# A decoder trunk on one core: other openings for the split products, an earlier norm statistic, and adaLN tables moved to TensorE

## The chip, the core and the metric

The kernel runs on one core of a Trainium2 chip. The engines spoken of are TensorE (PE in the profile; PEld is its weight load), VectorE (DVE), ScalarE (ACT), GpSimd (POOL) and SyncE (SP), which here issues most of the loads. Each engine runs its own instructions in the order in which the program gives them and waits on semaphores. The metric is the device time of one execution in microseconds; the profile's times count from the first instruction of the span.

## The reference

Two layers over 256 tokens of width 2048, all in float32. Layer 0 mixes tokens with an S5 state-space layer (128 groups of 16 channels, 64 complex states each), layer 1 with an RG-LRU; after each mixer stands a SwiGLU of hidden width 5632. Every sub-layer is normalised and modulated by the conditioning vector c.

```python
cond = jax.nn.silu(c)
for i in range(DEPTH):
    mod = cond @ w_ada[i] + b_ada[i]                 # 2048 -> 6 * 2048
    sh1, sc1, g1, sh2, sc2, g2 = [m[:, None, :] for m in jnp.split(mod, N_MOD, axis=-1)]
    h = rmsnorm(x, norm_g[i, 0]) * (1.0 + sc1) + sh1
    y = s5_mixer(h, ...) if i % N_MIXERS == 0 else rglru_mixer(h, ...)
    x = x + g1 * y
    h = rmsnorm(x, norm_g[i, 1]) * (1.0 + sc2) + sh2
    x = x + g2 * swiglu(h, ffn_w_gu[i], ffn_w_down[i])
return rmsnorm(x, final_g)
```

In the S5 mixer u = h @ w_in, then per group a diagonal complex recurrence over time with input and output matrices, a GELU, and y @ w_glu, whose halves are multiplied (value by sigmoid of gate).

## The kernel before

**One stream of weights.** All weights are read once, as 1 MB tiles (`raw`, four buffers, NRAW = 4) in one written order, the list `items` in `run`. `Stream.load` issues a load on SP's queue as soon as the program comes to a step; on the chip it waits until the buffer four items back is free. `Stream.step` (L443 on) uses an item up by its kind: "w" is a weight block that is split, "f" an S5 input block used as it is, "a", "p" and "q" are adaLN tables (192 of them, 128 columns of w_ada each).

**adaLN tables.** Kind "a" is one VectorE instruction per table (L486): multiply by c and sum, one output column. Kind "p" goes through TensorE: four tables hold four row blocks of 512 columns, each table gives four matmuls at once into four strips of a bank `pa` (L494); after the fourth, ScalarE copies the bank to `par` (L500), and at the next group's second table `rows_out` turns the rows into columns with four small matmuls into `pc` (L515) and a copy into `modr` (ScalarE L507, VectorE L505 once `late` is set). The string KINDS says which table is of which kind; the host lays the tables out by it.

**Split products.** A float32 product is made of two reduced-precision parts of each operand. For each 128 x 128 block of weights ScalarE makes the high part `wh` (L467) and VectorE the low part `wl` (L482); activations are kept as x[:, 0] high and x[:, 1] low, 256 columns each. `mac` (L586) issues a pair for one block: `wl` times the high activations (256 columns, L594), then `wh` times both (512 columns, L595). `product` runs 16 or 22 pairs into one bank. With `turn`, the first pair of a product is issued the other way round (L591, L592). In the kernel before, that is so in product g of j = 1 in the first half of each FFN, in lg5, in every xb from j = 2 on, and in wo2.

**The opening and the first mixer.** `s5_layer` (L817) first goes through tables, while VectorE makes the S5 parameter tables in the generator `prep` (16 pieces up to its yields, two pieces each step), ScalarE and POOL make the sum of squares of X (`sq_add`, L659 to L664), and POOL makes matrices of group t in `gen_gl(t)` (twelve instructions; it needs buffers s5gs, of which there are two). `norm_stat` (L667) has three parts: two matmul groups that sum over channels, then the variance on VectorE (`var_s`, L680) and its power on POOL (`rs_s`, L681), then a matmul that spreads it (`nrb_s`, L685). The norm is applied to X by sixteen VectorE multiplications (L877). `gen2(t)` has TensorE transpose and multiply what `gen_gl(t)` made: its bank `pt` has one buffer, is changed by VectorE (L323) and copied by ScalarE (L327). `gen_p(t)` makes phase tables on VectorE (L290 to L293; five buffers).

Then a loop over t = 0 to 15: 16 matmuls `in` (L891) of block t of w_in, and between them the pieces of neighbouring groups: states of t - 1 (`pv` L353, then a chain on VectorE with a scan, L362 to L372, ending in `S`), outputs of t - 2 (`py`, L390 and L392, which reads S), and gen2 of t + 2. Two adaLN tables follow each block from t = 1 on. At the end of each turn stand gen_d, gen_p, a small load and gen_gl.

**After it.** `glu` (v and gt products, 32 in all), `ffn` for layer 0 (two halves of 44 products g and u, then 16 products d of 22 pairs), `lru_layer` (44 products xb and lg with the block-diagonal gates `ri` between them, whose matmuls have 256 columns each, and 16 products wo), `ffn` for layer 1, and the last norm. In `modulate` the first two products of a stage run interleaved in two banks (f_first, lru_first).

Of the kernel before, what the change touches and what calls it, by code (L numbers as in the profile page):

```python
# [29 lines left out]
def bc(ap, axis, n):  # L30

    ap = ap.unsqueeze(axis)
    shape = list(ap.shape)
    shape[axis] = n
    return ap.to_broadcast(shape)


def weight_slots(pool):
# [364 lines left out]
class Stream:  # L403
# [138 lines left out]
    def next(self):  # L542

        if not self.pieces:
            self.ahead()
        self.cur = self.pieces.pop(0)
        return self.cur[0], self.cur[1]
# [23 lines left out]
class Model:  # L571
# [11 lines left out]
                self.side.pop(0)  # L583


    def mac(self, bank, w, x, first, last, turn=False):  # L586

        mm = self.nc.tensor.matmul
        wh, wl = w
        if first and turn:  # L590
            mm(bank, wh, x, start=True, stop=False, skip_group_check=True)  # L591
            mm(bank[:, 0], wl, x[:, 0], start=False, stop=False, skip_group_check=True)  # L592
        else:
            mm(bank[:, 0], wl, x[:, 0], start=first, stop=False, skip_group_check=True)  # L594
            mm(bank, wh, x, start=False, stop=last, skip_group_check=True)  # L595

    def product(self, ps, rhs, nk, name, last=False, turn=False):


        bank = self.bank(ps, name)  # L600
        for k in range(nk):
            self.mac(bank, self.st.next(), rhs(k), k == 0, k == nk - 1, turn)
            if last in (True, "hold") and k > nk - 10:
                self.st.delay = True
            self.st.used(last in ("hold", "evict") and k == nk - 1)
        return bank
# [156 lines left out]
    def ffn(self, layer, perm, nxt):  # L763
        nc, tc = self.nc, self.tc
        with ExitStack() as c:
# [6 lines left out]
            for half in range(2):  # L772
                for j in range(22):
                    nm = f"{layer}_{half}_{j}"
                    if j == 0 and half == 0:
                        bg, bu = first
                    else:
                        bg = self.product(ps, self.rhs_h, 16, f"g{nm}", turn=(half == 0 and j == 1))
                        bu = self.product(ps, self.rhs_h, 16, f"u{nm}")
                    g = hp.tile([P, T], F32, tag="g", bufs=2, name=f"gs{nm}")  # L780
                    u = hp.tile([P, T], F32, tag="u", bufs=2, name=f"us{nm}")
                    self.halves(hp, bg, g, f"g{nm}")
                    nc.scalar.activation(g, g, AF.Silu)  # L783
                    self.halves(hp, bu, u, f"u{nm}")
                    nc.vector.tensor_tensor(u, g, u, MUL)
                    self.split(hid[:, j], u)
                    self.pump()
                if half == 0:
                    g2 = self.mods(layer, 5)
                elif nxt:  # L790
                    self.scale(*nxt)
                for m in range(16):
                    nm = f"{layer}_{half}_{m}"
                    if half == 1 and m == 15:
                        self.sq_add(14)
                    bd = self.product(ps, lambda k: hid[:, k], 22, f"d{nm}", half == 1 and m == 15)
                    if half == 1 and 0 < m < 15:
                        self.sq_add(m - 1)
                        if not nxt and m - 1 in FIN_POOL:
                            nc.scalar.activation(self.X[:, m - 1], self.X[:, m - 1], AF.Copy,  # L800
                                                 scale=self.ng[:, 4, m - 1:m])
                    x = self.X[:, m]
                    t = hp.tile([P, T], F32, tag="dt", bufs=2, name=f"dt{nm}")
                    gm = g2[:, m:m + 1]
                    nc.vector.scalar_tensor_tensor(t, bd[:, 1], gm, x, MUL, ADD)
                    if perm and half == 1:
                        nc.vector.scalar_tensor_tensor(
                            x.rearrange("p (m q) -> p q m", q=4), bd[:, 0].rearrange("p (q m) -> p q m", q=4), gm,
                            t.rearrange("p (q m) -> p q m", q=4), MUL, ADD)
                    else:  # L810
                        nc.vector.scalar_tensor_tensor(x, bd[:, 0], gm, t, MUL, ADD)
                    self.pump()
                if half == 1:
                    self.sq_add(15)


    def s5_layer(self):  # L817
# [3 lines left out]
        with ExitStack() as c:  # L821
# [23 lines left out]
            with tc.tile_pool(name="s5prep", bufs=1) as pw:  # L845
# [7 lines left out]
                    s5.load_bc(t)  # L853
                prep = s5.prep(pw)
                stat = self.norm_stat(mm, "s5")
                for i in range(16):
                    st.step()
                    for _ in range(2):
                        next(prep, None)
                    if 2 <= i < 10:  # L860
                        self.sq_add(2 * i - 4, nc.gpsimd)
                        self.sq_add(2 * i - 3, nc.gpsimd)
                    if i == 10:
                        s5.gen_gl(0)
                    if 10 < i < 13:
                        next(stat)
                    if i == 13:
                        s5.gen_gl(1)
                for _ in prep:
                    pass  # L870
            s5.work = c.enter_context(tc.tile_pool(name="s5w", bufs=1))
            next(stat, None)
            for i in range(16, 28):
                st.step()
                if i < 20:
                    for k in range(4 * i - 64, 4 * i - 60):
                        nc.vector.tensor_tensor(self.X[:, k], self.X[:, k], self.rs, MUL)  # L877
                if 20 <= i < 25:
                    s5.gen_p(i - 20)
                if i in (17, 23):  # L880
                    for f in s5.gen2((i - 17) // 6):
                        f()
                    s5.gen_gl((i - 17) // 6 + 2)
            st.late = True
            s5.load_bc(4)
            s5.gen_d(0)
# [36 lines left out]
            for t in range(16):  # L923
# [25 lines left out]
                if t == 0:  # L949
                    nc.scalar.activation(self.cond, self.cond, AF.Silu)  # L950
                s5.gen_d(t + 1)
                if 0 < t < 11 or t == 14:
                    s5.gen_p(t + 4 if t < 11 else 15)
                s5.load_bc(t + 5)
                if t != 9:
                    s5.gen_gl(t + 4 if t < 9 else t + 3)
# [18 lines left out]
    def glu(self):  # L975
        nc, ps, d, g1 = self.nc, self.ps, self.d, self.mod[:, 32:48]
        with self.tc.tile_pool(name="glu", bufs=1) as wk:
# [10 lines left out]
                nc.vector.tensor_tensor(self.X[:, m], self.X[:, m], V.pop(m), ADD)  # L988
            V[0] = self.acc
            for m in range(1, 15):  # L990
                bv = self.product(ps, self.rhs_h, 16, f"v{m}")
                if m > 1:
                    self.sq_add(m - 2)
                gate(m - 1)
# [54 lines left out]
    def lru_layer(self):  # L1049
        nc, tc, d = self.nc, self.tc, self.d  # L1050
        v, s, e = nc.vector, nc.scalar, nc.gpsimd
        with ExitStack() as c:
# [78 lines left out]
                    R[i].clear()  # L1131

            def g0(j):
                G[j]["ps"] = self.product(ps, self.rhs_h, 16, f"lg{j}", turn=(j == 5))

            spare = []

# [26 lines left out]

            def x0(j):
                if j > 1:
                    first.append(self.product(ps, self.rhs_h, 16, f"xb{j}", "evict", True))

            def xe(j):
                x = xr[j % 2]  # L1170
# [36 lines left out]
            for m in range(16):  # L1207
                if m == 14:
                    self.scale(1, 1)
                if m == 15:  # L1210
                    self.sq_add(14)
                bd = wo[m] if m < 2 else self.product(ps, lambda k: dst[k], 22, f"wo{m}", m == 15, m == 2)
                if 0 < m < 15:
                    self.sq_add(m - 1)
                x = self.X[:, m]
# [103 lines left out]

FIN_POOL = (2, 4, 6, 8, 10, 12)  # L1320

KINDS = "p" * 32 + "p" * 8 + "a" * 40 + "qqqp" + "a" * 56 + "qqqp" + "a" * 32 + "qqqp" + "a" * 12


def lru_ks(j):
# [95 lines left out]
```

## Time and profile before

| what | value |
|---|---|
| time, median of 3 runs | 2520.15 us (2510.43 to 2521.91) |
| profiled execution, its own time | 2520.73 us |
| its span | 2518.6 us, 36646 instructions |
| PE busy | 2393.6 us, 95% of the span |
| DVE busy | 1933.3 us, 77% |
| ACT, POOL busy | 1297.6 us (52%), 351.6 us (14%) |
| read from HBM | 614.57 MB, 245 GB/s over the span |
| mean granted TensorE clock | 0.977 |

"Busy" of PE counts a matmul until its modelled end, so neighbouring matmuls overlap and a PE without a gap shows as fully busy. A row of waits reads: engine, line waiting <- engine, line that ended the wait: us in total, times, longest. A row of one line's instructions reads: how many, shortest/median/longest duration in ns, first and last start. In groups the number behind the first bar is busy us, then mean ns of one, then idle time before it. A timeline row reads: start, us, engine, line, operation.

### The profile page before, as it was taken

Reading aid. Unit: us, or ns where it says so; the run is one execution under the profiler, and the core shown is the slowest. Engines: PE = TensorE matmul, PEld = TensorE weight load, DVE = VectorE, ACT = ScalarE, POOL = GpSimd, SP = SyncE. Lnnn points to the kernel's source line nnn. Section 1 sums busy time; section 2 is a strip of 40 time slices with the busy share of each in tenths; the row PEclk is TensorE's granted clock in tenths of the full one; section 3 lists DMA queues with packets and bytes.
Section 4 is the critical chain, followed back from the end, with each engine's and each line's share of the span. In section 5 each row is a group of like instructions: output and inputs, shape, how many; then the busy total and the mean of one; then the engine's idle time right before and its main releaser. Section 6 shows DMA issues by size and latency. Waiting matters only on the chain. (4 is left out here: it accounts for less than half of the span.)

```text
span 2518.6 us, 36646 instructions
## 1 busy us (share of the span) xinstructions
PE 2393.6 (95%) x14120; PEld 2054.9 (82%) x14120; DVE 1933.3 (77%) x2653; ACT 1297.6 (52%) x2520; POOL 351.6 (14%) x345
## 2 busy tenths in 40 slices
PE   5697898999999999999999988999999999999998
PEld 1276787887888888888888887888788888888887
DVE  9669887887776787777889999888777555555565
ACT  1286675445444444444446765554645444454443
POOL 5579530001000000000003333010100000000000
PEclk9799898999999999999999999999999999999999
DMA  9744555887676798776886446879777556555553
GB/s 379 283 180 176 186 207 227 322 311 279 248 258 232 269 329 322 279 282 251 307 312 222 158 157 241 316 276 324 293 285 262 182 179 209 201 199 188 172 192 134
DMA packets 98415, 619.04 MB, mean 246 GB/s; under 512 B 11201, under 2 KB 15681, under 8 KB 38977
## 3 DMA queue, kind: packets, MB, share of 16 engines
q1 hardware_dynamic: 96368, 613.04, 67.3%
q10 hardware_dynamic: 1872, 3.67, 0.4%
q8 instruction: 110, 1.80, 0.3%
q14 instruction: 65, 0.52, 0.1%
HBM read 614.57 MB, written 2.10 MB: 245 GB/s over the span
## 5 line engine op out<-in xcount | busy, mean ns | idle before, releaser
L482 DVE TENSOR_TENSOR wl<-raw,wh 128x1024 fp32r<-128x1024 f32 (+2 forms) x824 | 888.2, 1099 | 350.7 <-ACT wh L467 347.6
L467 ACT ACTIVATE wh<-raw 128x1024 fp32r<-128x1024 f32 (+2 forms) x824 | 769.6, 952 | 677.7 <-PE d L595 194.6
L595 PE MATMUL d<-hid,wh 128*128 128x512 f32 x1408 | 483.6, 391 | 0.0
L595 PE MATMUL u<-H,wh 128*128 128x512 f32 x1376 | 476.5, 390 | 0.0
L595 PE MATMUL g<-H,wh 128*128 128x512 f32 x1374 | 475.8, 391 | 0.0
L594 PE MATMUL d<-hid,wl 128*128 128x256 f32 x1408 | 391.4, 278 | 0.0
L594 PE MATMUL u<-H,wl 128*128 128x256 f32 x1376 | 382.5, 278 | 0.0
L594 PE MATMUL g<-H,wl 128*128 128x256 f32 x1374 | 382.0, 278 | 0.0
L486 DVE CUSTOM_DVE_ANT_0 raw<-raw,cond 128x2048 f32<-128x2048 f32 x140 | 327.3, 2343 | 1.1 <-DMA raw<-in_wada 0.8
L595 PEld LDWEIGHTS d<-hid,wh 128*128 128x128 f32 x1408 | 264.2, 188 | 56.8
L595 PEld LDWEIGHTS u<-H,wh 128*128 128x128 f32 x1376 | 258.3, 188 | 55.3
L595 PEld LDWEIGHTS g<-H,wh 128*128 128x128 f32 x1374 | 257.8, 188 | 55.0
L594 PEld LDWEIGHTS d<-hid,wl 128*128 128x128 f32 x1408 | 264.3, 188 | 0.0
L594 PEld LDWEIGHTS u<-H,wl 128*128 128x128 f32 x1376 | 258.3, 188 | 0.0
L594 PEld LDWEIGHTS g<-H,wl 128*128 128x128 f32 x1374 | 258.0, 188 | 0.1
L891 PE MATMUL in<-s5h,raw 128*128 128x256 f32 x512 | 149.5, 413 | 7.6 <-DMA raw<-in_s5win 6.3
L783 ACT ACTIVATE gs<-gs 128x256 f32<-128x256 f32 x88 | 36.8, 418 | 202.3 <-DVE gs L632 202.3
L595 PE MATMUL lg<-H,wh 128*128 128x512 f32 x351 | 124.2, 398 | 0.0
L891 PEld LDWEIGHTS in<-s5h,raw 128*128 128x128 f32 x512 | 91.2, 201 | 23.7 <-issue 7.8
L594 PE MATMUL lg<-H,wl 128*128 128x256 f32 x351 | 99.6, 284 | 4.5 <-DVE wl L482 4.5
L595 PE MATMUL xb<-H,wh 128*128 128x512 f32 x300 | 103.4, 390 | 0.0
L681 POOL TENSOR_TENSOR rs_lru<-var_lru,mhalf 128x2 f32<-128x2 f32 x1 | 1.6, 1600 | 729.1 <-DVE var_lru L680 729.1
(381 smaller groups left out, 3651.3 us busy)
## 6 DMA issues: line engine op xcount, KB each, us to landing
raw<-in_wada SPq DMA_DIRECT2D x192, 1024.0 KB, 5.5
raw<-in_gu SPq DMA_DIRECT2D x176, 1024.0 KB, 4.9
raw<-in_dn SPq DMA_DIRECT2D x128, 704.0 KB, 4.2
raw<-in_lruin SPq DMA_DIRECT2D x44, 1024.0 KB, 5.0
raw<-in_s5glu SPq DMA_DIRECT2D x32, 1024.0 KB, 5.6
raw<-in_lruout SPq DMA_DIRECT2D x32, 704.0 KB, 4.9
raw<-in_s5win SPq DMA_DIRECT2D x16, 1024.0 KB, 5.8
raw<-in_lruri SPq DMA_DIRECT2D x8, 512.0 KB, 5.4
```

What stands on the lines that cost most here:

```text
L467: nc.scalar.activation(dh, src, AF.Copy)
L482: self.nc.vector.tensor_tensor(*self.lazy.pop(0), SUB)
L486: self.nc.vector.tensor_tensor_reduce(t, t, self.cond, 1.0, 0.0, MUL, ADD, self.mod[:, n:n + 1])
L594: mm(bank[:, 0], wl, x[:, 0], start=first, stop=False, skip_group_check=True)
L595: mm(bank, wh, x, start=False, stop=last, skip_group_check=True)
L681: nc.gpsimd.tensor_tensor(rs, var, self.mhalf, ALU.pow)
L783: nc.scalar.activation(g, g, AF.Silu)
L891: nc.tensor.matmul(bank, st.next()[0], hf[:, k], start=(k == 0), stop=(k == 15))
```

## The change

Three edits. First, `product` takes a tuple: an order for each of its first pairs. Order 0 issues the high part as two matmuls of 256 columns and then the low part; order 1 issues the high part (512) and then the low part (256). `every(m)` gives orders (0, 1) to the first two pairs when m % 4 == 1. It is used for g in both halves of both FFNs, for d, for v, for lg, and, shifted by three, for wo; xb gets order 1 for its first pair at j = 2, 6, 10, 14 and 18 only.

Second, KINDS makes tables 40 to 59 of kind "p"; they stand behind the S5 input blocks of the loop over t.

Third, in the opening the squares are taken in steps 1 to 3 and the first two parts of `norm_stat` at step 6, ahead of that step's pieces of `prep`; gen_gl 0 and 1 are issued at steps 7 and 9; the spreading matmul follows step 13 instead of step 15; gen2 stands at steps 16 and 21 instead of 17 and 23; and two of the five gen_p there go into the loop over t.

```diff
+def every(m):
+    return (0, 1) if m % 4 == 1 else ()
...
-    def mac(self, bank, w, x, first, last, turn=False):
+    def mac(self, bank, w, x, first, last, turn=None):
...
-        if first and turn:
-            mm(bank, wh, x, start=True, stop=False, skip_group_check=True)
-            mm(bank[:, 0], wl, x[:, 0], start=False, stop=False, skip_group_check=True)
+        if turn == 0:
+            mm(bank[:, 0], wh, x[:, 0], start=first, stop=False, skip_group_check=True)
+            mm(bank[:, 1], wh, x[:, 1], start=False, stop=False, skip_group_check=True)
+            mm(bank[:, 0], wl, x[:, 0], start=False, stop=last, skip_group_check=True)
+        elif turn == 1:
+            mm(bank, wh, x, start=first, stop=False, skip_group_check=True)
+            mm(bank[:, 0], wl, x[:, 0], start=False, stop=last, skip_group_check=True)
         else:
...
-            self.mac(bank, self.st.next(), rhs(k), k == 0, k == nk - 1, turn)
+            self.mac(bank, self.st.next(), rhs(k), k == 0, k == nk - 1, turn[k] if k < len(turn) else None)
...
-                        bg = self.product(ps, self.rhs_h, 16, f"g{nm}", turn=(half == 0 and j == 1))
+                        bg = self.product(ps, self.rhs_h, 16, f"g{nm}", turn=every(j))
...
-                    bd = self.product(ps, lambda k: hid[:, k], 22, f"d{nm}", half == 1 and m == 15)
+                    bd = self.product(ps, lambda k: hid[:, k], 22, f"d{nm}", half == 1 and m == 15, every(m))
...
-                for i in range(16):
+                for i in range(14):
                     st.step()
+                    if i == 6:
+                        next(stat)
+                        next(stat)
                     for _ in range(2):
                         next(prep, None)
-                    if 2 <= i < 10:
-                        self.sq_add(2 * i - 4, nc.gpsimd)
-                        self.sq_add(2 * i - 3, nc.gpsimd)
-                    if i == 10:
-                        s5.gen_gl(0)
-                    if 10 < i < 13:
-                        next(stat)
-                    if i == 13:
-                        s5.gen_gl(1)
+                    if 1 <= i < 4:
+                        for k in range(6 * i - 6, min(6 * i, 16)):
+                            self.sq_add(k, nc.gpsimd)
+                    if i in (7, 9):
+                        s5.gen_gl((i - 7) // 2)
                 for _ in prep:
                     pass
+            next(stat, None)
             s5.work = c.enter_context(tc.tile_pool(name="s5w", bufs=1))
-            next(stat, None)
-            for i in range(16, 28):
+            for i in range(14, 28):
                 st.step()
-                if i < 20:
-                    for k in range(4 * i - 64, 4 * i - 60):
+                if i < 18:
+                    for k in range(4 * i - 56, 4 * i - 52):
                         nc.vector.tensor_tensor(self.X[:, k], self.X[:, k], self.rs, MUL)
-                if 20 <= i < 25:
-                    s5.gen_p(i - 20)
-                if i in (17, 23):
-                    for f in s5.gen2((i - 17) // 6):
+                if i in (16, 21):
+                    for f in s5.gen2((i - 16) // 5):
                         f()
-                    s5.gen_gl((i - 17) // 6 + 2)
+                    s5.gen_gl((i - 16) // 5 + 2)
+                if 22 <= i < 25:
+                    s5.gen_p(i - 22)
...
-                if 0 < t < 11 or t == 14:
-                    s5.gen_p(t + 4 if t < 11 else 15)
+                if t < 12 or t == 14:
+                    s5.gen_p(t + 3 if t < 12 else 15)
...
-                bv = self.product(ps, self.rhs_h, 16, f"v{m}")
+                bv = self.product(ps, self.rhs_h, 16, f"v{m}", turn=every(m))
...
-                G[j]["ps"] = self.product(ps, self.rhs_h, 16, f"lg{j}", turn=(j == 5))
+                G[j]["ps"] = self.product(ps, self.rhs_h, 16, f"lg{j}", turn=every(j))
...
-                    first.append(self.product(ps, self.rhs_h, 16, f"xb{j}", "evict", True))
+                    first.append(self.product(ps, self.rhs_h, 16, f"xb{j}", "evict", (1,) if j % 4 == 2 else ()))
...
-                bd = wo[m] if m < 2 else self.product(ps, lambda k: dst[k], 22, f"wo{m}", m == 15, m == 2)
+                bd = wo[m] if m < 2 else self.product(ps, lambda k: dst[k], 22, f"wo{m}", m == 15, every(m + 3))
...
-KINDS = "p" * 32 + "p" * 8 + "a" * 40 + "qqqp" + "a" * 56 + "qqqp" + "a" * 32 + "qqqp" + "a" * 12
+KINDS = "p" * 60 + "a" * 20 + "qqqp" + "a" * 56 + "qqqp" + "a" * 32 + "qqqp" + "a" * 12
```

More of the change, by code (lines that the diff above doesn't have):

```diff
@@ L595, in mac, with product @@
             mm(bank, wh, x, start=False, stop=last, skip_group_check=True)
-    def product(self, ps, rhs, nk, name, last=False, turn=False):
+    def product(self, ps, rhs, nk, name, last=False, turn=()):
         bank = self.bank(ps, name)
         for k in range(nk):
-            self.mac(bank, self.st.next(), rhs(k), k == 0, k == nk - 1, turn)
+            self.mac(bank, self.st.next(), rhs(k), k == 0, k == nk - 1, turn[k] if k < len(turn) else None)
             if last in (True, "hold") and k > nk - 10:
```

## The prediction

> **What bounds the kernel now.** I read the busy time by stage first, choosing the stretches by the code: opening (0 to 116.89 us), first mixer's loop over t (116.89 to 377.10), GLU, first FFN, recurrent layer, second FFN. Columns: stretch, its length, busy us (and count) of PE, weight loads, DVE, ACT, POOL, then granted clock, DMA share, GB/s.
>
> ```profile
> 0.00:61.70 61.70, 37.41 (x160) 10.80 (x160) 57.60 (x156) 10.38 (x27) 34.61 (x47) 0.99 0.96 385
> 61.70:78.69 16.99, 3.15 (x16) 1.52 (x20) 13.96 (x49) 0.00 (x0) 3.79 (x7) 0.50 0.03 11
> 78.69:116.89 38.20, 27.34 (x193) 9.97 (x185) 25.84 (x41) 14.87 (x49) 33.02 (x31) 0.81 0.95 378
> 144.02:190.14 46.12, 46.12 (x349) 36.76 (x345) 35.87 (x41) 36.61 (x148) 37.99 (x37) 1.00 0.56 215
> 190.14:203.26 13.12, 13.12 (x100) 11.73 (x97) 10.13 (x11) 12.26 (x52) 10.87 (x9) 1.00 0.58 239
> 364.42:377.10 12.68, 11.99 (x73) 10.62 (x73) 12.13 (x16) 9.04 (x26) 0.00 (x0) 1.00 0.72 255
> 190.14:377.10 186.96, 160.03 (x1013) 139.51 (x1009) 163.89 (x170) 130.61 (x533) 112.52 (x92) 0.90 0.53 191
> 600.00:1320.00 720.00, 720.00 (x4156) 634.00 (x4157) 559.95 (x721) 335.72 (x493) 0.00 (x0) 1.00 0.78 281
> 1340.00:1550.00 210.00, 194.85 (x1235) 176.37 (x1234) 202.08 (x309) 145.66 (x241) 61.62 (x59) 0.98 0.51 183
> 1800.00:2500.00 700.00, 700.00 (x4119) 619.78 (x4118) 443.59 (x573) 336.94 (x492) 0.00 (x0) 1.00 0.60 206
> ```
>
> Four readings. The opening runs at the rate of its loads, 385 and 378 GB/s, except for 17 us in which almost nothing is loaded (11 GB/s). The loop is all PE while its tables go through TensorE (46.12 of 46.12), and is not once they go through VectorE: 27 us of PE idle and a clock of 0.90. Both FFNs are PE without a gap. Yet one pair of matmuls (256 columns by the low part, 512 by the high) does not take equally long in the two FFNs; rows of one line: count, duration min/median/max in ns, first and last start.
>
> ```profile
> L595 PE MATMUL d<-hid,wh x318: 392/392/392, 839.9 to 949.8; 128*128 128x512 f32 x159
> L595 PE MATMUL d<-hid,wh x325: 389/389/389, 2029.6 to 2139.8; 128*128 128x512 f32 x163
> ```
>
> 109.9 us over 317 steps is 346.7 ns a pair; 110.2 over 324 is 340.1. The clock is 1.00 and the instructions are the same, so PE has a slow and a fast cadence, 6.67 ns apart, and keeps whichever it is in: in the trace the slow one holds for 2,076 pairs of the first FFN and the fast one for 2,078 of the second. A modelled duration of 392 or 389 ns marks them, which lets me read single stretches:
>
> ```profile
> L595 PE MATMUL gt<-H,wh x234: 392/392/392, 416.9 to 569.8; 128*128 128x512 f32 x117
> L595 PE MATMUL f_first<-H,wh x15: 389/389/398, 594.4 to 599.1; 128*128 128x512 f32 x15
> L595 PE MATMUL g<-H,wh x12: 392/392/392, 601.8 to 605.6; 128*128 128x512 f32 x12
> L595 PE MATMUL xb<-H,wh x260: 389/389/567, 1355.7 to 1507.7; 128*128 128x512 f32 x130
> L595 PE MATMUL lg<-H,wh x16: 392/392/393, 1513.6 to 1518.8; 128*128 128x512 f32 x16
> L595 PE MATMUL lg<-H,wh x189: 392/392/392, 1574.8 to 1640.0; 128*128 128x512 f32 x189
> L595 PE MATMUL wo<-H,wh x16: 389/389/391, 1671.2 to 1676.3; 128*128 128x512 f32 x16
> L595 PE MATMUL wo<-H,wh x192: 392/392/392, 1678.7 to 1767.8; 128*128 128x512 f32 x192
> L595 PE MATMUL f_first<-H,wh x16: 392/392/399, 1790.6 to 1795.8; 128*128 128x512 f32 x16
> L595 PE MATMUL g<-H,wh x14: 389/389/389, 1797.7 to 1802.2; 128*128 128x512 f32 x14
> ```
>
> The cadence changes where the old kernel opened a product with the high part: between f_first and g in both FFNs (once to slow, once to fast) and in wo2 (to fast; wo3 fell back by itself). After the gates' 256 column matmuls (ri), such an opening (xb) always ended fast, while lg0, opened low part first, ended slow.
>
> **Part 1: the openings.** The new opening is three 256 column matmuls, then high 512, low 256, low 256, high 512. Of all stretches in the trace it is most like an xb behind ri:
>
> ```profile
> 1355.06 0.28 PE L1092 MATMUL ri<-yext,wrl 128*128 128x256 f32 x1
> 1355.18 0.40 PE L591 MATMUL xb<-H,wh 128*128 128x512 f32 x1
> 1355.41 0.28 PE L592 MATMUL xb<-H,wl 128*128 128x256 f32 x1
> 1355.53 0.28 PE L594 MATMUL xb<-H,wl 128*128 128x256 f32 x1
> 1355.65 0.39 PE L595 MATMUL xb<-H,wh 128*128 128x512 f32 x1
> ```
>
> I therefore forecast fast. What is unknown is whether three matmuls settle what a dozen of ri do; both ends are kept (all fast, all slow). Price of one opening: three times 0.12 us for a 340 ns pair, +0.02, and the high-first step, another +0.02 (0.23 against 0.227 for the high, 0.12 twice against 0.113): 0.04 us. There are 54 (FFNs 40, v 4, lg 6, wo 4): 2.2 us. Slow pairs within reach: first FFN 2,076; GLU 348 of some 480, since v1 runs at the throttled start and I count only from v5; lg some 285 behind lg5; wo 220 behind wo6. 2,929 pairs by 6.67 ns is 19.5 us. The xb lose 15 of 20 old openings; slow again they cost 15 x 16 x 6.67 ns = 1.6 us, of which I take 0.5 because DVE is busy 202 of 210 us there and hides part (bounds 0 and 1.6). Sum 19.5 - 2.2 - 0.5 = **-16.8 us**. All slow instead: the second FFN loses 2,078 x 6.67 = 13.9, plus 2.2 and 1.3: +17.4.
>
> [...]
>
> **Part 2: tables 40 to 59 on TensorE.** Removed from DVE in the loop:
>
> ```profile
> L486 DVE CUSTOM_DVE_ANT_0 raw<-raw,cond 128x2048 f32<-128x2048 f32 x20 | 52.6, 2664 | 0.0
> PE py L392 <- DVE S L371: 13.2, 4, 6.7
> ```
>
> 52.6 us of 163.9 DVE us; the scan's S, for which PE waits, stands behind them. Added: 20 x 4 matmuls on PE, five times four for the columns, a row copy on ACT and a small DVE copy for each four tables. The trace shows this mode: three turns with two TensorE tables each take 46.12 us, 15.37 a turn; the turn without any takes 13.12. So two tables cost PE 2.25 us. New loop from 190.14: eight turns at 15.37, two without gen_gl at 12.68 + 2.25, the last at 12.68: 165.5 against 186.96, **-21.5 us**. DVE then has 111 us of work in it and POOL 112, so neither binds; ACT's added copies (five of 0.6 us) lie under 131 of 187. Bounds: this is nearly the good end, since PE has no gap left in that mode; if all stalls stay, the tables are pure cost, 10 x 2.25, +22.5.
>
> **Part 3: the opening.**
>
> ```profile
> PE nrb_s L685 <- POOL rs_s L681: 19.2, 1, 19.2
> 43.52 2.68 POOL L274 TENSOR_TENSOR gm<-s5bc,s5al 128x640 f32<-128x640 f32 x2
> 51.40 2.10 POOL L279 TENSOR_TENSOR s5gs<-gm,gm 64x384 f32<-64x384 f32 x2
> 43.80 1.36 DVE L159 TENSOR_TENSOR prm<-e 128x128 f32<-128x128 f32 x1
> 52.66 1.09 DVE L159 TENSOR_TENSOR prm<-b 128x128 f32<-128x128 f32 x1
> 64.93 0.39 DVE L159 TENSOR_TENSOR prm<-e 128x128 f32<-128x128 f32 x1
> 67.47 0.39 DVE L159 TENSOR_TENSOR prm<-p 128x128 f32<-128x128 f32 x1
> 74.48 0.15 DVE L680 TENSOR_SCALAR var_s<-nrm_s 128x2 f32<-128x2 f32 x1
> L877 DVE TENSOR_TENSOR X<-X,nrb_s 128x256 f32<-128x256 f32 x16 | 5.5, 415 | 2.2 <-issue 2.2
> L327 ACT ACTIVATE s5T<-pt 32x128 f32<-32x128 f32 (+3 forms) x32 | 7.3, 227 | 3.8 <-DVE pt L323 3.5
> L293 DVE TENSOR_TENSOR s5pt<-s5pt,pm 128x512 f32<-128x512 f32 x5 | 6.3, 1269 | 0.2
> ```
>
> The 17 us without loads are this wait: PE stands at nrb, the tables behind it hold their buffers. Now var follows the 12th of prep's 16 pieces. That wait goes; what is late next? The eight DVE steps from 43.80 to 52.66 took 8.9 us beside the eight long POOL operations of the first gen_gl, and their likes from 64.93 took 2.5 without. So var comes at 46.3, and from 47 POOL does rs and then gen_gl 0, 1 and 2 in a row, some 11.3 us each with their copies, all beside the rest of prep (71 instructions, 21.8 us undisturbed). About 13 get through per gen_gl, 45 by 81, the other 26 by 89. Twelve scalings of X (5.5 us per 16) and the pt operation follow at 93.3, ACT's sixteen s5T copies (7.3 us per 32) end at 97, and only then does PE pass gen2(1), which now stands at step 21. PE is thus held from about 70, with 26 items of 33 loaded instead of 20. First load again at about 99; seven MB at 378 GB/s (2.77 us each) end at 118.4, thirteen from 78.69 end at 114.7: **+3.7 us**. Bounds: DVE undisturbed gives prep's end at 67.5, loads from 77.3, -18; a slower hold (PE clock 0.50 as in 61.70:78.69, fewer DVE steps) +7. The two gen_p moved into turns 0 and 1 (three operations of 1.27 us each) lie under PE: even turns 2 to 4, with the whole scan, leave DVE 10 of 46 us free; uncovered they cost 7.6. Squares in three steps instead of eight keep ACT's first row copy back by about 1 us, hidden by four buffers of loads.
>
> **Sum.** The profiled execution took 2520.73 us (span 2518.6), 0.6 above the median of 2520.15, so the median is forecast the same way: 2520.7 - 16.8 - 21.5 + 3.7 = 2486.1, **2486**. The lowest of the three runs is 10 us under the others, as 1,500 pairs of the other cadence would make it.
>
> **Rivals.** *Loads run through* (DVE less disturbed beside POOL than its eight steps at 43.80): opening -18, 2464. For it: X's sixteen scalings took 0.34 us each though half of them ran beside POOL; against: prep's own rows. *Each opening flips the cadence*, as the old ones did between f_first and g and in wo2: half of the pairs everywhere fast, 9.8 - 6.9 - 2.2 - 0.5 = 0 from part 1, 2503; against: the xb. *All end slow*: +17.4, 2520; for it: lg0 behind ri. *The stalls stay* (the other side): turns stall not for the reduces but for gen_gl beside DVE's scan; then part 2 costs 22.5 us and the sum is 2530, slower than before; it decides from a loop of 200 us on (13 more than now). Against it: the three turns at 46.12 had the same gen_gl and no PE gap. *Order is worth nothing*: the openings' price alone, 2.2 + 0.5, 2506.
>
> **Chances.** Forecast 0.45 (own range 2476 to 2497), loads run through 0.17, flips 0.15, nothing 0.06, all slow 0.09, stalls stay 0.05; 0.03 outside. Range 2462 to 2510: it holds the first four. Within 0.5% (12.6 us) counts as no change, about what can be told: faster 0.82, same 0.14, slower 0.04.
>
> **What would show it.** Right: the first FFN's high matmuls at 389 ns; no DVE reduce before the GLU, turns of about 15.4 us with PE full and clock 1.00; no PE wait for rs, but one at gen2(1) near 70 to 97 with loads stopped. Wrong: 392 ns rows in the second FFN, turns over 16 us, loads without a gap.

## The result, and the profile after

The changed kernel takes 2496.6 us (median of 8 runs, 2491.7 to 2500.8); the kernel before, over 8 runs, 2509.9 us (2505.7 to 2521.9). The ratio is 0.9941, with an interval of 0.9920 to 0.9962: faster by 0.4 to 0.8%, about 13 us, which is little more than the 0.5% below which the prediction counts a change as none. The forecast was 2486 us, its own range 2476 to 2497. The profiled execution of the changed kernel took 2500.8 us, its span is 2499.0, 19.6 us under that of before.

The table cuts both spans at the same matmuls: the first `in`, the first `in` of t = 5, the end of the first matmul behind the loop, the first `v`, f_first, lru_first and the f_first of layer 1. Three experiments, which are told below, stand beside them.

| stretch, us | before | after | openings alone | tables alone | both, old start |
|---|---|---|---|---|---|
| opening, to the first `in` | 116.9 | 134.3 | 120.1 | 120.9 | 117.1 |
| loop, t = 0 to 4 | 73.2 | 75.8 | 75.9 | 74.0 | 75.6 |
| loop, t = 5 to 15 | 187.0 | 165.3 | 183.6 | 165.3 | 165.3 |
| end of loop to the first `v` | 33.5 | 31.3 | 33.5 | 31.6 | 31.2 |
| GLU | 175.4 | 172.0 | 171.2 | 172.4 | 171.1 |
| first FFN | 741.7 | 731.4 | 729.2 | 730.2 | 729.9 |
| recurrent layer | 454.1 | 453.1 | 450.7 | 454.0 | 450.8 |
| second FFN and end | 736.8 | 735.7 | 737.3 | 750.0 | 736.6 |

So the products gained 15.8 us (GLU to end, forecast 16.8), the loop with its end 23.9 (forecast 21.5), and the opening with the turns up to t = 4 lost 20.0, where 3.7 were forecast. The busy time by stretch of the changed kernel, columns as in the prediction:

```profile
0.00:134.35 134.35, 63.33 (x365) 22.27 (x365) 110.47 (x238) 25.91 (x76) 68.68 (x84) 0.75 0.72 289
...
69.71:104.59 34.88, 1.99 (x12) 0.59 (x16) 28.76 (x63) 4.30 (x18) 15.05 (x17) 0.56 0.18 75
...
210.14:375.47 165.33, 165.33 (x1214) 133.90 (x1211) 113.77 (x142) 133.98 (x547) 100.39 (x92) 1.00 0.56 220
600.00:1300.00 700.00, 700.00 (x4134) 620.49 (x4132) 553.64 (x713) 329.66 (x484) 0.00 (x0) 1.00 0.78 286
...
1780.00:2480.00 700.00, 700.00 (x4136) 620.59 (x4135) 443.33 (x572) 336.64 (x491) 0.00 (x0) 1.00 0.58 207
```

The loop is PE from end to end (165.33 of 165.33) at a clock of 1.00, and VectorE has 114 us of work in it where it had 164. The hole without loads is still there, only later and longer: from one issue of a load to the next it is 35 us (69.71 to 104.59), where it was 22 us in the kernel before (56.45 to 78.69; the 17 us of the prediction are the part of it in which almost nothing arrived). The high matmuls of the products u, one row for each FFN:

```profile
L605 PE MATMUL u<-H,wh x687: 388/389/389, 599.7 to 1181.5; 128*128 128x512 f32 x172
L605 PE MATMUL u<-H,wh x672: 388/389/389, 1793.8 to 2365.1; 128*128 128x512 f32 x168
```

Both FFNs now hold the fast cadence, but for 65 pairs of products d (1227 to 1250 us). Over the whole trace 4,980 pairs are fast and 545 slow, by the time from one high matmul to the next; before it was 2,408 and 3,247. And the waits of the opening, from 60 to 135 us:

```profile
PE pa L499 <- ACT par L505: 36.0, 2, 32.9
ACT s5T L332 <- DVE pt L328: 32.5, 1, 32.5
POOL s5gs L274 <- PE pt L326: 24.2, 1, 24.2
DVE pt L328 <- ACT s5G L318: 10.8, 1, 10.8
```

PE does not stand at gen2(1), as forecast, but at a table: `pa` of tables 20 to 23 waits for the row copy `par` of tables 16 to 19 on ScalarE. ScalarE stands with the s5T copies of gen2(0), which wait for VectorE's pt. VectorE had this order of work:

```profile
93.78 4.05 DVE L886 TENSOR_TENSOR X<-X,nrb_s 128x256 f32<-128x256 f32 x12
97.76 0.25 DVE L328 SCALAR_TENSOR_TENSOR pt<-s5id,s5dsk,pt 128x32 f32<-128x32 f32 x1
...
110.14 0.26 DVE L328 SCALAR_TENSOR_TENSOR pt<-s5id,s5dsk,pt 128x32 f32<-128x32 f32 x1 [10.81 <-ACT s5G L318]
```

And ScalarE behind it:

```profile
98.04 3.82 ACT L332 ACTIVATE s5T<-pt 32x128 f32<-32x128 f32 x16 [32.51 <-DVE pt L328]
101.88 0.17 ACT L512 ACTIVATE modr<-pc 128x4 f32<-128x4 f32 x1
101.95 0.59 ACT L505 ACTIVATE par<-pa 128x512 f32<-128x512 f32 x1
```

The `par` copy itself takes 0.6 us; it is late because of what stands ahead of it in its queue. At 111.58 the copies of gen2(1) put themselves ahead of the next `par` in the same way.

### The profile page after: what moved, and what is told of

It reads as the page before. It is cut to its first block, busy times and chain, and to the rows that moved or that the text cites. A ratio compares the mean times of both kernels' runs of the same rounds, so it can differ in the third digit from the quotient of the medians.

```text
span 2499.0 us, 37144 instructions
## 1 busy us (share of the span) xinstructions
PE 2379.5 (95%) x14374; PEld 2045.1 (82%) x14374; DVE 1895.4 (76%) x2618; ACT 1298.4 (52%) x2525; POOL 339.3 (14%) x345
## 5 line engine op out<-in xcount | busy, mean ns | idle before, releaser
L605 PE MATMUL d<-hid,wh 128*128 128x512 f32 x1376 | 469.3, 389 | 0.0
L605 PE MATMUL g<-H,wh 128*128 128x512 f32 x1328 | 455.7, 389 | 0.0
L604 PE MATMUL d<-hid,wl 128*128 128x256 f32 x1376 | 380.1, 276 | 0.0
L604 PE MATMUL g<-H,wl 128*128 128x256 f32 x1328 | 366.7, 276 | 0.0
L605 PEld LDWEIGHTS g<-H,wh 128*128 128x128 f32 x1328 | 249.3, 188 | 50.8
L491 DVE CUSTOM_DVE_ANT_0 raw<-raw,cond 128x2048 f32<-128x2048 f32 x120 | 274.7, 2290 | 3.6 <-DMA raw<-in_wada 3.6
L604 PEld LDWEIGHTS g<-H,wl 128*128 128x128 f32 x1328 | 249.2, 188 | 0.9
L499 PE MATMUL pa<-raw,condz 128*32 128x512 f32 x576 | 87.5, 714 | 70.7 <-ACT par L505 45.6
L605 PE MATMUL xb<-H,wh 128*128 128x512 f32 x315 | 110.9, 395 | 0.0
L499 PEld LDWEIGHTS pa<-raw,condz 128*32 128x32 f32 x576 | 14.8, 118 | 110.9 <-ACT par L505 52.8
L900 PEld LDWEIGHTS in<-s5h,raw 128*128 128x128 f32 x512 | 87.9, 195 | 19.6 <-issue 11.1
```

The source lines that it names most:

```text
L491: self.nc.vector.tensor_tensor_reduce(t, t, self.cond, 1.0, 0.0, MUL, ADD, self.mod[:, n:n + 1])
L499: nc.tensor.matmul(self.bank[32 * c:32 * c + 32], self.condz[:, 4 * q + c], t[:, 512 * c:512 * c + 512], start=(q == 0), stop=(q == 3), ti ...
L900: nc.tensor.matmul(bank, st.next()[0], hf[:, k], start=(k == 0), stop=(k == 15))
```

## The experiments

My theory after the result: the openings set the cadence, the tables free VectorE in the loop, and the opening is worse because a chain VectorE (prep, X, pt), ScalarE (s5T, par), PE (tables) now holds the loads. The main rivals: that the cadence falls as it will and the openings were only lucky; that the new start costs nothing and the loss lies in chance; that POOL or the loads themselves set the opening. Each kernel's ratio is against runs of the kernel before on the same chip. Differences in us to the changed kernel are between medians of different sessions, in which the median of the kernel before lay between 2507.7 and 2515.9 us; taken from the ratios, the same differences come out up to 5 us otherwise.

**The three edits one at a time.** The kernel before with the tuple orders alone (`mac`, `product` and the calls as in the change):

```diff
+    return (0, 1) if m % 4 == 1 else ()
...
+                        bg = self.product(ps, self.rhs_h, 16, f"g{nm}", turn=every(j))
```

> Only the new orders of the first two pairs of every fourth product; opening and tables as before. Theory: every such opening leaves PE in the fast cadence (389 ns for the 512 column matmul, 340.0 ns a pair), so the time falls by about 16 us against the kernel before, nearly all of it in GLU (-3), first FFN (-10 to -13) and wo (-1); the second FFN, fast already, stays within 1.5 us. Rival: the fast cadence came with the other edits (another start moves every later event), the rows stay at 392 ns in the first FFN and the time moves by less than 4 us.

Measured: 2502.9 us (2497.9 to 2510.8, 12 runs), ratio 0.9956 (0.9938 to 0.9975): 12.9 us under the median of before in the same session, 2515.9, where about 16 were expected. Its trace has 5,227 fast pairs and 291 slow.

The kernel before with KINDS alone:

```diff
-KINDS = "p" * 32 + "p" * 8 + "a" * 40 + "qqqp" + "a" * 56 + "qqqp" + "a" * 32 + "qqqp" + "a" * 12
+KINDS = "p" * 60 + "a" * 20 + "qqqp" + "a" * 56 + "qqqp" + "a" * 32 + "qqqp" + "a" * 12
```

> Only tables 40 to 59 by TensorE. Theory: the loop's turns 5 to 14 take 15.0 to 16.0 us with PE full, 24 us less from turn 5 to the GLU, and the time falls by about 22 to 24 us. Rival: the loop gains only because the two gen_p's went into it or because VectorE enters it later; then the stalls of 20 to 28 us stay in some turns and the gain is under 12 us.

Measured: 2492.2 us (2482.9 to 2502.8), ratio 0.9907 (0.9873 to 0.9940), 23.7 us. From t = 5 on its loop is that of the changed kernel:

```profile
194.88:360.20 165.32, 165.32 (x1214) 133.88 (x1211) 109.80 (x139) 134.63 (x547) 99.41 (x92) 1.00 0.56 220
```

This trace says something on the cadence too. It has the old openings, and yet its first FFN is fast (up to 1173 us) and its second slow, the other way round than in the trace of before:

```profile
L595 PE MATMUL u<-H,wh x658: 389/389/389, 599.7 to 1165.8; 128*128 128x512 f32 x165
L595 PE MATMUL u<-H,wh x656: 392/392/392, 1791.2 to 2362.1; 128*128 128x512 f32 x164
```

With the old openings an FFN can fall into either cadence, in kernels whose FFNs are the same; one FFN in the other cadence is 13.9 us (2,078 pairs by 6.67 ns). It fits that the three runs that the prediction started from lay 11 us apart and that their median stood 10 us above that of eight; the cadence of the runs without a trace was not seen.

The kernel before with the new start alone, the change's third edit with its gen_p:

```diff
+                    if i == 6:
+                        next(stat)
+                        next(stat)
...
+                if i in (16, 21):
...
+                if t < 12 or t == 14:
+                    s5.gen_p(t + 3 if t < 12 else 15)
```

> Only the new order of the opening. Theory: PE is held from about 70 to 102 us because ScalarE's copy of a table bank stands behind the s5T copies, which wait for VectorE's pt at the end of prep; turn 1 begins 16 to 20 us later than before, and the time rises by 14 to 20 us. Rival: the delay is of the profiled execution (VectorE's first copy there lost 10 us against POOL's memsets) and of the tables together; alone the time rises by less than 6 us or falls.

Measured: ratio 1.0043 (1.0018 to 1.0067): slower by about 11 us, less than the 14 to 20 expected. Its first `in` comes at 134.35 us, to the hundredth where the changed kernel has it, and turn 1 begins 20.1 us later than in the kernel before. (Both FFNs are in the slow cadence in its trace, 741.7 and 750.1 us.)

Openings and tables with the old start, the changed kernel with these lines taken back:

```diff
-                for i in range(14):
+                for i in range(16):
...
-                if i in (16, 21):
+                if i in (17, 23):
```

> Openings and tables as in the changed kernel, the opening's order as before (five gen_p there). Theory: the parts add up, so it is 36 to 41 us faster than before and 16 to 20 us faster than the changed kernel. Rival: without the later start VectorE enters the loop with less done, turns grow and half of the gain goes; 20 to 28 us faster than before.

Measured: 2483.7 us (2479.7 to 2489.0), ratio 0.9875 (0.9848 to 0.9902). Two of the three edits are worth 32 us, and the third takes 13 of them away (2496.6 - 2483.7; 17 by the ratios). By the medians both are less than the theory's 36 to 41 and 16 to 20.

**What an opening does to the cadence.** Its two halves were tried apart.

```diff
-    return (0, 1) if m % 4 == 1 else ()
+    return (1,) if m % 4 == 1 else ()      # high part first only
+    return (0,) if m % 4 == 1 else ()      # three 256 column matmuls only
```

> The changed kernel, with every fourth product opened high part first (512 columns, then the low 256) but without the pair of three 256 column matmuls ahead of it. Theory A: such an opening alone flips the cadence, as it did between f_first and g in the kernel before; then stretches of four products alternate between 392 and 389 ns, some 2,300 more pairs are slow, and the median rises by 12 to 16 us less 1 for the cheaper openings, to 2508 to 2512. Theory B: the order alone ends fast whatever stood before: over 4,900 pairs of 389 ns, 2494 to 2497. Theory C: it ends slow: both FFNs at 750 us, 2522 to 2528.

Measured: 2512.0 us, 15.4 above the changed kernel. Three successive stretches between openings in the first FFN:

```profile
L605 PE MATMUL u<-H,wh x64: 392/392/394, 638.9 to 677.4; 128*128 128x512 f32 x64
L605 PE MATMUL u<-H,wh x64: 388/389/389, 683.2 to 721.0; 128*128 128x512 f32 x64
L605 PE MATMUL u<-H,wh x64: 392/392/394, 726.9 to 765.3; 128*128 128x512 f32 x64
```

It goes on like this through both FFNs: each such opening turns the cadence over (2,736 pairs slow, 2,837 fast). Theory A holds; high part first is not what makes it fast.

> The changed kernel, with the other half of the opening alone: every fourth product begins with the three 256 column matmuls (high, high, low) and goes on low part first, without the pair that is issued high part first. Theory (the three matmuls set the cadence, high part first flips it): each opening ends in the slow cadence, as lg0 did behind the 256 column matmuls of ri; under 900 of some 5,600 pairs stay fast (the xb are still opened high part first), both FFNs take 741 to 751 us, and the median is 26 to 31 us over that of the changed kernel, at 2522 to 2528. Rival 1: three such matmuls leave the cadence as it is; then it is decided elsewhere, one FFN or both may be fast, and executions scatter by 10 us and more around 2505 to 2515. Rival 2: they alone end fast: 2494 to 2498.

Measured: 2529.5 us, 32.9 above the changed kernel and slower than before (ratio 1.0074, 1.0055 to 1.0094). 5,229 pairs are slow, 289 fast; the FFNs take 742.2 and 750.6 us:

```profile
L605 PE MATMUL u<-H,wh x560: 392/392/394, 684.7 to 1189.5; 128*128 128x512 f32 x187
...
L605 PE MATMUL u<-H,wh x688: 392/392/394, 1794.9 to 2388.5; 128*128 128x512 f32 x172
```

So the three 256 column matmuls set a known state, the slow one, and the pair behind them, high part first, turns it over: in these traces, at a granted clock of 1.00, (0, 1) is fast every time, (0) slow every time, (1) alternates, and without an opening either came out. In the changed kernel 52 of the 54 openings are followed by fast pairs; the two others, those of v1 and lg1, began at a throttled clock (granted 0.50 from 406.3 to 408.0 us and 0.59 from 1509.1 to 1511.0).

**What holds the opening.** First the two places in the chain. Only the s5T copies of gen2(0) are moved, from step 16 to behind step 20:

```diff
-                    for f in s5.gen2((i - 16) // 5):
+                    parts = s5.gen2((i - 16) // 5)
+                    late = parts.pop() if i == 16 else None
+                    for f in parts:
                         f()
...
+                if i == 20:
+                    late()
```

> The changed kernel, with only ScalarE's sixteen s5T copies of gen2(0) moved from step 16 to behind step 20, so that the row copy of tables 16 to 19 stands ahead of them; gen2(1) at step 21 still needs them. Theory: the hold moves from step 20 to gen2(1) at step 21, as the prediction had it; one or two more items are loaded before the loads stop, the first `in` comes 3 to 6 us earlier than in the changed kernel (at 128 to 131 us where the first s5id copy is long, as in its profile, at 123 to 126 where it is short), and the median falls by 2 to 6 us, to 2491 to 2495. Rival: something else holds PE at the same place (the one pt bank, POOL), and the first `in` and the median stay within 1.5 us of 134.3 (long) or 129.1 (short) and of 2496.6.

Measured: 2491.2 us (2487.5 to 2494.5), 5.4 under the changed kernel; the first `in` at 128.95 with the same long first copy. By then 26 loads are issued, as the prediction had it, where the changed kernel has 24; the loads still stop for 31 us (74.8 to 105.8). The hold is now where the prediction had put it:

```profile
PEld pt L326 <- ACT s5T L332: 24.8, 1, 24.8
PE pt L326 <- ACT s5T L332: 24.4, 1, 24.4
```

Then gen2 behind the tables:

```diff
-                if i in (16, 21):
-                    for f in s5.gen2((i - 16) // 5):
+                if i in (25, 27):
+                    for f in s5.gen2((i - 25) // 2):
                         f()
-                    s5.gen_gl((i - 16) // 5 + 2)
+                    s5.gen_gl((i - 25) // 2 + 2)
```

> The changed kernel, with gen2(0) and gen2(1) (and the gen_gl behind each) moved from steps 16 and 21 of the opening to steps 25 and 27; nothing else is changed. Theory: the loads stop because ScalarE's row copy of the tables stands behind the s5T copies, which wait for VectorE's pt, which stands behind prep; with gen2 behind the last tables nothing that the tables need waits for prep, so the loads run on without a gap of over 5 us, the first `in` matmul comes at 100 to 108 us instead of 134.3, turn 1 starts at 118 to 125 instead of 150.3, and the median falls by 24 to 30 us, to 2467 to 2473. Rival 1: VectorE itself is what the opening ends on (prep, X, then pt), so that the first `in` comes after 120 and the gain is under 14 us (above 2482). Rival 2: gen_gl(2) and gen_gl(3) come too late now and turns 2 and 3 wait for POOL: turn 1 is early, but turn 5 starts less than 15 us earlier than in the changed kernel (210.1).

Measured: 2474.3 us (2471.1 to 2475.8), 22.4 under the changed kernel. The gain falls just short of the 24 to 30 expected, and the loads do not run through as the theory had it: the first `in` comes at 111.15, and loads still pause, from 86.6 to 107.6, now behind the last tables. pt(0) runs at 99.25 though X is done at 88.6: three gen_p (steps 22 to 24) stand ahead of it on VectorE, and the first `in` stands behind gen2(1). Not all of the gain is gen2's: gen_gl(2) moves with it, so that prep has less POOL work beside it: X begins at 83.2, where it begins at 90.1 in a trace of the changed opening with an equally short first copy (told below).

The old start, with every wait moved behind the tables (spread, X, gen2(0) at steps 24 to 27, gen2(1) two steps on, and all gen_p but two in the loop), together with openings and tables:

```diff
+                if i == 24:
+                    next(stat, None)
+                    for f in s5.gen2(0):
+                        f()
+                    s5.gen_gl(2)
+                if i >= 24:
+                    for k in range(4 * i - 96, 4 * i - 92):
+                        nc.vector.tensor_tensor(self.X[:, k], self.X[:, k], self.rs, MUL)
```

> The kernel of openings and tables with the old opening, in which the spreading matmul of the norm, gen2(0) with gen_gl(2) and the scaling of X move to steps 24 to 27, gen2(1) with gen_gl(3) behind the two steps that follow, and gen_p(2) to gen_p(4) into the loop. Theory: as in the changed kernel with gen2 late, no table waits for VectorE or POOL, the 17 us without loads go, the first `in` comes at 98 to 106 us instead of 117.1, and the median is 12 to 20 us under that of the old opening with openings and tables (2483.7), at 2464 to 2472. Rival: what was waited for in the middle is waited for at the end, since the statistic (74.5 us before) is followed by rs, spread, 16 scalings of X and pt on one VectorE: under 6 us gained.

Measured: 2467.1 us (2458.1 to 2470.2), ratio 0.9798 (0.9750 to 0.9845), 16.6 under the old start. It is the fastest of all here. Its opening against that of gen2 late:

```profile
0.00:101.54 101.54, 64.20 (x364) 21.41 (x364) 88.52 (x233) 23.35 (x72) 60.05 (x78) 0.74 0.97 392
```

392 GB/s and a DMA share of 0.97 over the whole opening: here the loads bind, as the opening before did only outside its hole (385 and 378 GB/s). gen2 late had 0.84 and 336 GB/s up to its first `in`.

**Why VectorE is late: POOL beside it.** The first three gen_gl are left out:

```diff
-        if t >= 16:
+        if t >= 16 or t < 3:
             return
```

> The changed kernel without the POOL work of gen_gl(0), gen_gl(1) and gen_gl(2): the input and output matrices of groups 0 to 2 are left out, the rest is as it is. Theory: prep is slow because nearly each VectorE operation ends only with the long POOL operation beside it; without them the last piece of prep ends at 70 to 76 us instead of 93.8, ScalarE's s5T copies end by 84 instead of 101.9, the stop of the loads shrinks from 35 us to under 15, the first `in` comes at 108 to 118 instead of 134.3, and the median falls by 16 to 26 us (2471 to 2481). Rival: prep is slow by its own waits (ScalarE, its loads): its end stays above 88, and the median within 6 us of 2496.6.

Measured: 2474.0 us (2472.9 to 2475.2), 22.7 under the changed kernel. X follows at once on prep, so that its first scaling marks prep's end; the changed kernel, then this one:

```profile
L886 DVE TENSOR_TENSOR X<-X,nrb_s x16: 408/410/415, 93.8 to 98.9; 128x256 f32<-128x256 f32 x16
```

```profile
L886 DVE TENSOR_TENSOR X<-X,nrb_s x16: 414/418/422, 70.5 to 75.7; 128x256 f32<-128x256 f32 x16
```

Prep ends 23 us earlier. In this trace the first copy, told below, is shorter, and var comes 1.6 us earlier for it; so nearly 22 us of prep are time lost beside gen_gl. The stop of the loads shrinks to 13 us (68.3 to 81.4). The seam shows in the changed kernel where gen_gl begins; VectorE, the same line before and in it:

```profile
50.22 0.23 DVE L174 TENSOR_SCALAR prm<-prm 128x64 f32<-128x64 f32 x1
...
52.84 1.27 DVE L174 TENSOR_SCALAR prm<-prm 128x64 f32<-128x64 f32 x1
54.15 1.36 DVE L175 TENSOR_TENSOR p<-p,prm 128x128 f32<-128x128 f32 x1
```

**The first copy.** In the changed kernel's trace VectorE started its parameter tables late:

```profile
1.37 12.21 DVE L139 COPY s5id<-ident 32x32 f32<-32x32 f32 x4
...
19.68 0.20 DVE L187 TENSOR_SCALAR r<-r 128x64 f32<-128x64 f32 x1
```

The first of the four copies took 11.65 us. In other traces, of kernels with the same instructions up to there, the four take 5.17 us; high part first alone is one, and its `in` comes at 129.1:

```profile
1.38 5.17 DVE L139 COPY s5id<-ident 32x32 f32<-32x32 f32 x4
...
6.58 1.12 DVE L59 TENSOR_SCALAR prm<-s5lam 128x64 f32<-128x64 f32 x1
...
15.99 0.20 DVE L187 TENSOR_SCALAR r<-r 128x64 f32<-128x64 f32 x1
```

POOL fills buffers with zeros all that time, from 1.25 to 13 us. To see whether that is the cause, ScalarE made the zeros:

```diff
-            nc.gpsimd.memset(x, 0.0)
...
+            nc.scalar.activation(x, zero.to_broadcast([P, x.shape[1]]), AF.Copy)
```

> The changed kernel, with the thirteen zero fills at the start (s5gs, s5ls, s5d, s5T) made by ScalarE copies of a zero column instead of POOL memsets; nothing else changes. Theory (VectorE's first s5id copy is long, 11.65 us, because POOL's memsets beside it keep it waiting): the four copies take under 0.3 us each and VectorE's sixteen small operations behind them 0.2 us each, so that VectorE has r ready near 9 us instead of 16 to 19.9. ScalarE's fills take some 10 to 13 us behind its 3.9 us start, so its first sine comes at 15 to 18 us, var at 46 to 49 us instead of 50.8, the first `in` at 128 to 132 instead of 134.3, and the median falls by 0 to 5 us (2491.5 to 2496.6). Rival: the first copy is long by itself or by what it waits for (the identity, a load), and stays at 1.7, 7.3 or 11.7 us.

Measured: 2488.6 us (2486.1 to 2489.5), 8.0 under the changed kernel, more than expected, and a spread of 3 us in place of 9. VectorE:

```profile
1.38 0.16 DVE L143 COPY s5id<-ident 32x32 f32<-32x32 f32 x1
1.56 0.55 DVE L143 COPY s5id<-ident 32x32 f32<-32x32 f32 x3
...
9.45 0.19 DVE L191 TENSOR_SCALAR r<-r 128x64 f32<-128x64 f32 x1
```

The copies take 0.17 us each and r is ready 10.2 us earlier. ScalarE's sine waits for ScalarE's own fills until 16.42, but VectorE uses that time for its next operations, which I had not counted: var comes at 42.7 instead of 50.8, and the first `in` at 127.3.

## Why the prediction was right or wrong

**Right in sign; 10.6 us too low** against the median, 14.7 against the profiled execution. Two of its three terms held, and the third failed. That the number came so near is in part luck: a gain of 34 us was forecast, and between the medians of eight runs it is 13; the base, the median of three runs, stood 10 us above that of eight.

**Part 1, the openings (-16.8).** Measured -15.8 from GLU to end in the two traces. What it rested on, that three matmuls settle what a dozen of ri do, is shown by the two halves: without the three, cadences alternate; with them alone, all is slow. The rivals "each opening flips" and "all end slow" are thus true statements on half an opening each, and their prices came out: 15.4 and 32.9 us over the changed kernel. "Order is worth nothing" is out, since the openings alone took 12.9 us off. At a granted clock of 1.00 the pairs in these traces come in two cadences, every 340.1 or every 346.7 ns. The first FFN gained 10.3 of the 13.0 forecast (2,076 pairs, less twenty openings), GLU 3.4 for 2.3 less its openings. Leaving v1 out because of the throttled start was right (its 256 columns took 415 ns, where a later opening's take 281): it ended slow, and the eight products up to v5 stayed so. xb and lg together were to gain 1.4 (lg 1.9, less 0.5 for the xb) and went from 310.0 to 310.5 us: lg has 237 slow pairs fewer, but xb 168 more, which is 1.1 us where 0.5 was put. wo's own matmuls gained 1.8 us (123.1 to 121.3), where 1.5 was forecast before its openings. The rest, about 1 us in xb and lg, was not followed. The weak point is the base: "slow in the first FFN, fast in the second" was that execution's draw, as the tables alone show with the reverse. Against an execution of before with both FFNs fast, the part's own terms leave 3 us (19.5 - 13.8 - 2.2 - 0.5).

**Part 2, the tables (-21.5).** Forecast 165.5 us from 190.14; measured 165.3, in every trace that has the tables, to 0.01 us. Part of this closeness is luck: the first eight turns took 124.2 us (forecast 123.0), the other three 41.2 (forecast 42.5). The rest of the 23.9 is the end of the loop to `v`, 2.2 us, which the prediction left out. "The stalls stay" is out: no turn stalls.

**Part 3, the opening (+3.7).** This is the step that failed, measured +20.0, and the new start alone is slower than before. The mechanism was the one named (prep late beside gen_gl, then X, pt, s5T, PE held with the loads stopped), and so were most of its times where the first copy was short: var at 47.05 for 46.3, prep's end at 90.1 for 89, pt at 94.05 for 93.3. What it got wrong is the sentence "only then does PE pass gen2(1), which now stands at step 21" with "26 items of 33 loaded". I followed PE's queue and not ScalarE's: behind the s5T copies stands `par`, so PE stops two tables earlier, at table 20 and not behind 21, with 24 items.

Of the 16.3 us that are missing, that step is 5.4 (the copies late, same first copy); the long first copy, which the prediction could not know, up to 5.2 (134.35 against the 129.14 of high part first alone, which has the same opening; but three 256 alone, with that opening and the long copy, has 132.19, so that both these figures are uncertain by 2 us); the longer turn t = 0 is 2.5 and is hardly the edit's, since that turn took 14.1 to 16.1 us with the old start in the three traces of the table and 13.4 only in that of before. It goes with the clock granted in that turn: 13.4 us at 0.94 in the kernel before, 15.9 at 0.76 in the changed one, 13.2 at 0.95 with three 256 alone. What sets the clock there stays open. The other 3 are left; the second hold, behind the copies of gen2(1) from 111.6, where PE stands 3.1 us, lies in them, but was not measured by itself. The bounds (-18 to +7) did not hold the value: both ends were worked out with the hold at gen2(1), and neither had the long copy or the longer turn in it.

"Loads run through" was the right aim of the edit and not what it did; two kernels with other orders come nearer to it.

## What to carry to other kernels

When a step is moved, follow the queue of every engine that it issues on, and ask for each what stands behind it: here a 0.6 us row copy on ScalarE stood behind copies that wait for VectorE, and the loads stopped with it. Putting that one copy ahead shortened the stop only from 35 to 31 us, since the next step waited for the same late parameters. Work that waits for late parameters belongs behind the last work that frees load buffers. And a state that an engine can fall into and keep, like the cadence here, is to be read in several traces before its gain is counted; better, it is set.

## What the runs showed of the hardware that was not expected

TensorE's cadence for pairs of 256 and 512 columns is kept from pair to pair. In these traces, at a granted clock of 1.00, three 256 column matmuls lead to the slow one (346.7 ns a pair), one pair issued high part first turns it over (340.1 ns), and the pairs behind keep it, for a whole FFN in some traces (2,076 pairs in the first FFN of the kernel before). It is not kept for certain: in the middle of a product d, with no opening there, the fast cadence fell to the slow one at 1226.4 us in the changed kernel, whose next opening set it right 65 pairs later, and at 1173.2 us with the tables alone, which stayed slow for the other 328 pairs of that FFN. With the clock throttled at its start (256 columns in 415 ns; granted 0.50 in the changed kernel) an opening can end the other way: v1 in the changed kernel went on slow (392 ns), and v1 with the three matmuls alone, 415 ns too, went on fast (389 ns). In openings alone the GLU took 171.2 us, 0.8 less than in the changed kernel; by my estimate that is v1 to v5 in the fast cadence (128 pairs by 6.67 ns, 0.85 us). The opening of v1 in the changed kernel, then the v pairs with the three matmuls alone:

```profile
L597 PE MATMUL v<-H,wh x1: 415/415/415, 406.7 to 406.7; 128*128 128x256 f32 x1
```

```profile
L605 PE MATMUL v<-H,wh x74: 389/389/612, 402.6 to 449.8; 128*128 128x512 f32 x74
```

Why an opening can end otherwise at a throttled start, and why the fast cadence falls, is open.

VectorE beside POOL: a copy of 32 x 32 takes 0.17 us alone, 1.13 beside POOL's zero fills, and in the worst case 11.65, until the last fill is done (the copy ends at 13.03 us, the fill at 13.00); which of them an execution gets is not in the program: of the twelve traces with POOL's fills five have the long copy, among them the changed kernel's, five the short one (1.75 us), and two one of 7.29. In the kernel before, which has the short case, the four copies and the three operations behind them each end 0.03 to 0.05 us after one of POOL's fills (0.95 to 1.20 us each); in the changed kernel the first copy outlasts all fifteen. Why a copy ends with one fill in some executions and only with the last in others is open.
